# A trunk of gated attention layers: the value projections of two attentions as seven block products, values parked in DRAM, and a softmax difference in one operation

## The chip, the cores and the metric

The kernel runs on one core of a Trainium2 chip. The metric is the time of one execution on the device, in microseconds (us). Before the change, three runs gave 1922.32 us (median), 1922.04 us (lowest) and 1923.9 us (highest).

The engines are named as in the profile: PE is the matrix engine (TensorE), PEld its loading of the stationary operand, DVE the vector engine, ACT the scalar engine, POOL is GpSimd and SP is SyncE, which issues nearly all DMAs of this kernel.

## What is computed

Two layers over 512 tokens of width 1024. Each layer mixes tokens by three branches on the same input, and then applies a SwiGLU block that the change doesn't touch. Cut to what matters:

```
x                                     # (512, 1024)
in-projection of x:                   # one weight matrix w_in, column ranges
    rq, rk, rv, rg                    # retention: 512, 512, 1024, 1024 columns
    cq, ck, cv                        # chunked attention: 512 columns each, 8 heads of 64
    dq, dk, dv                        # differential attention: 512 columns each, 4 heads of 128
    gates                             # 3 branches x 1024 columns
A = retention(rq, rk, rv) * silu(rg)
B = chunked attention: softmax(cq ck' + bias) cv          # per head, under a triangle of chunks
C = differential attention, per head with two score matrices S0 and S1:
    o = (softmax(S0) - lam * softmax(S1)) dv
    o = o / sqrt(mean(o^2) + eps) * g * (1 - lambda_init)
mix = sum over branches of sigmoid(gate) * (branch @ w_branch)
x   = layer_norm(alpha * x + mix @ w_out)
```

## The kernel before

Every projection is made in three passes (lines 122, 123, 124): a float32 operand is split into a high part and a rest (tiles `wh` and `wl` for weights, `xTh` and `xTl` for the input), and high x high, rest x high and high x rest are added up in PSUM. The high part is a cast on ACT (line 106, or line 151 for weights that `Wt` loads and line 225 for those of `Halves`), the rest a subtraction on DVE (line 112, 152, 226). A matmul of the kernel mostly has 128 rows, a stationary operand of 128 columns and 512 moving columns.

The body of a layer is a hand-written list of items (at the end of the layer function). An item is one projection, with the weights that it needs, and up to a few groups of attention steps: the steps stand between the parts of the projection, so that PE has matmuls of the projection to do while ACT and DVE work on a softmax. Weights are loaded three items ahead (`AHEAD`) into three slots (`NSTAGE`). Engines take their instructions in the order in which the list and a recorder of the program put them; waits between engines go by semaphores. The items are:

- `u_gate(br, i)`: 256 gate columns, a tanh on ACT (line 965) into a tile `th`; the ones in `EARLY` are made long before use, stored to DRAM and loaded again.
- `u_rvg(hp)`: for one half of the retention heads, the 512 value and the 512 gate columns together as a product of a 2x2 block of inputs with a 2x2 block of weights, with seven block products in place of eight (Winograd's form: items m1, y, x, m2, v, g, h). `Halves` loads the weights' four quarters of 1 MB and makes the sums of quarters on DVE (line 182); `Quarters` holds the sums of the input's quarters. Each of the seven is 2 x 12 matmuls into banks named `pf`.
- `u_vhl(dst, base, wd)`: the 512 value columns of the chunked attention (`cv`) or the differential attention (`dv`) in the direct way, 4 x 24 matmuls into banks named `pn`. Each row block is cast and split into tiles `vhl`, where high part and rest of a head lie side by side.
- `u_cqk(p)`, `u_dqk(h)`: queries and keys of two heads of the chunked, or of one head pair of the differential attention, 24 matmuls for the queries and 24 for the keys. For the differential attention both are turned by `rotary` (lines 313 to 317): four copies `sw` on ACT, three operations on DVE; then `set_q` and `set_k` cast on ACT (`qs`, `ks`) and subtract on DVE (`kl`).
- `u_branch(br, i)`: 256 columns of a branch's output, multiplied by the gate and added up (lines 995 and 999).

The attention steps of the chunked attention are `s_c1` (scores into `psc`, maximum on DVE and exponential with sums on ACT at lines 363 and 365, then reciprocal and four multiplications of the tiles `cE` by it on DVE, line 829), `s_c2` (ten transposes into `ptr`, line 378, then casts `cPh` and rests `cPl`), and `s_c3` (product with the values, banks `pco`, line 854, a copy `cos` and an addition `cot`). Those of the differential attention are `s_d0(h, j)` for the two score matrices (lines 363, 365, reciprocal at 886, times -lam at 888), `s_d1` after the second (lines 901 and 902: for each of four row blocks, one multiplication of the second softmax and one operation that scales the first and adds), `s_d2` (ten transposes of `dE`, casts `dPh`), `s_d3` (product with the values, banks `pdo`, lines 927 to 944, with copies `do`, squares `junk` and the root mean square) and `s_d4` (four transposes `pdt`, line 954, and a split into `och` and `ocl`, which the last branch reads). The functions `c(i)` and `d(i)` say which steps belong to the i-th step of the pipeline: d(i) scores head i // 2 while the head before is transposed and multiplied.

In the list, the pairs of d steps stand with `u_gate(1, i)` and `u_branch(1, i)`, and between two pairs stands `u_dqk(h)` with no step at all:

```
(u_gate(1, 0), *d(0)), (u_branch(1, 0), *d(1)), (u_dqk(1),),
(u_gate(1, 1), *d(2)), (u_branch(1, 1), *d(3)), (u_dqk(2),),
```

Of the kernel before, what the change touches and what calls it, by code (L numbers as in the profile page):

```python
# [17 lines left out]
P = 128  # L18
# [25 lines left out]

EARLY = [(0, 0), (0, 1), (0, 2), (0, 3), (2, 0), (2, 1)]

# [10 lines left out]
def trunk(ctx, tc, x_in, xT_in, w_in, ret_norm_g, da_norm_g, lq1, lk1, lq2, lk2, w_a, w_b, w_c, b_merge, w_out,  # L57
# [100 lines left out]
    class Halves:  # L158
# [16 lines left out]

        def parts(self):
            h = max(self.kh // 2, 1)
            return [slice(a, min(a + h, self.kh)) for a in range(0, self.kh, h)]

        def add(self, t, u):  # L180
            for s in self.parts():
                nc.vector.tensor_add(t[:, s], t[:, s], u[:, s])

        def block(self, t):
            return Staged(t, self.kh, self.parts())

# [29 lines left out]
    class Staged:  # L216


        def __init__(self, st, nk, parts):
            n = 512 * nk  # L220
            self.nk = nk
            self.hi = wsp.tile([P, 2048], F32R, tag="wh", name="wh")[:, :n].rearrange("p (k c) -> p k c", k=nk)
            self.lo = wsp.tile([P, 2048], F32R, tag="wl", name="wl")[:, :n].rearrange("p (k c) -> p k c", k=nk)
            for s in parts:
                nc.scalar.copy(self.hi[:, s], st[:, s])  # L225
                nc.vector.tensor_sub(self.lo[:, s], st[:, s], f(self.hi[:, s]))  # L226

# [298 lines left out]
    def layer(l):  # L526
# [128 lines left out]

        def u_rvg(hp):

            hv = Halves(W, 0, 4, (RV + 512 * hp, RG + 512 * hp))
            t = {}
# [14 lines left out]
            def x(j, ps):  # L674
                u, y = g(name="tu"), t["y", j]
                t["u", j] = u
                nc.vector.tensor_sub(u, ps, t["m", j])
                nc.vector.tensor_add(y, y, u)

            def m2(j, ps):  # L680
                c = t.pop(("m", j))
                nc.vector.tensor_add(c, c, ps)
                rv_done(hp, j, c)

            def v(j, ps):
                c = g(name="tv")
                nc.vector.tensor_add(c, t["y", j], ps)
                rg_done(hp, j, c)

            def g_(j, ps):  # L690
                c, u = t.pop(("y", j)), t["u", j]
                nc.vector.tensor_add(c, c, ps)
                nc.vector.tensor_add(u, u, ps)
                rg_done(hp, 2 + j, c)

            def h(j, ps):
                u = t.pop(("u", j))
                nc.vector.tensor_sub(u, ps, u)
                rv_done(hp, 2 + j, u)

# [74 lines left out]

        def u_vhl(dst, base, wd):

            def fn(*wts):
                for t in range(NT):
                    ps = bank("pn")  # L780
                    proj_N(xT, wts, t, ps)
                    for hf in range(2):
                        s = g(F32R, "vhl")
                        dst[t, hf] = s
                        s3 = s.rearrange("p (h x) -> p h x", x=2 * wd)
                        src = ps[:, 256 * hf:256 * hf + 256].rearrange("p (h x) -> p h x", x=wd)
                        part_hi(s3[:, :, 0:wd], src)
                        part_lo(s3[:, :, wd:2 * wd], src, s3[:, :, 0:wd])
                    between()
            return rows_of(W, base), fn  # L790

# [22 lines left out]
        def s_c1(h):  # L814
            def fn():
# [10 lines left out]
                for nt in range(NT):  # L826
                    pk, c = PACK[NT - 1 - nt]
                    e = E[pk][:, c:c + P * (nt + 1)]
                    nc.vector.tensor_scalar_mul(e, e, r[:, nt:nt + 1])
                cE[h] = E  # L830
# [50 lines left out]
        def s_d0(h, j):  # L881
            def fn():
                e = [g(name="dE") for _ in range(3)]
                sums = softmax_num(dqk[h], j, tabs["mask"], e)
                r = small.tile([P, NT], F32, tag="rec", name="rec")
                nc.vector.reciprocal(r, sums)
                if j:
                    nc.vector.tensor_scalar_mul(r, r, v["nlam"])
                dE[h, j] = e, r
                if j:  # L890
                    s_d1(h)()
            return fn

        def s_d1(h):
            def fn():
                (E0, R0), (E1, R1) = dE.pop((h, 0)), dE.pop((h, 1))
                E, R = (E0, E1), (R0, R1)
                for nt in range(NT):
                    pk, c = PACK[NT - 1 - nt]
                    cs = slice(c, c + P * (nt + 1))  # L900
                    nc.vector.tensor_scalar_mul(E[1][pk][:, cs], E[1][pk][:, cs], R[1][:, nt:nt + 1])
                    nc.vector.scalar_tensor_tensor(E[0][pk][:, cs], E[0][pk][:, cs], R[0][:, nt:nt + 1],
                                                   E[1][pk][:, cs], op0=ALU.mult, op1=ALU.add)
                dE[h] = E[0]
            return fn

        def s_d2(h):
            def fn():
                dP[h] = triangle("dP")
                transpose_triangle(dE.pop(h), dP[h])  # L910
            return fn

        def s_d3(h):
            def fn():
                pT = dP.pop(h)
                ss = small.tile([P, NT], F32, tag="ss", name="ss")
# [103 lines left out]

        p, q = u_rvg(0), u_rvg(1)
        for (specs, fn), *groups in [
            (u_first(),), (u_gate(0, 1), [s_q(0)], [s_q(1)]), (p["m1"], [], [s_q(2)]),
            (u_gate(0, 2), [s_q(3)], [s_r1(0)]), (p["y"],), (p["x"],), (u_gate(0, 3), [], [s_r1(1)]), (p["m2"],), (p["v"],),
            (u_gate(2, 0),), (p["g"],), (p["h"],),
            (u_rqk(rq, RQ, 1), [], [s_r2(0)]), (q["m1"],), (u_rqk(rk, RK, 1), [s_r2(1)], [s_r3(0)]), (q["y"], [], [s_r3(1)]),
            (u_gate(2, 1),), (q["x"],), (q["m2"],), (q["v"],), (q["g"],), (q["h"],),
            (u_vhl(cv, CV, 64), [s_r1(2)], [s_r1(3)], [s_r2(2)], [s_r2(3)]), (u_cqk(0), [s_r3(2)], [s_r3(3)]),
            (u_branch(0, 0), *c(0)), (u_cqk(1), *c(1)), (u_branch(0, 1), *c(2)), (u_cqk(2), *c(3)),
            (u_branch(0, 2), *c(4)), (u_cqk(3), *c(5)), (u_branch(0, 3), *c(6)),  # L1030
            (u_vhl(dv, DV, 128), *c(7), *c(8)), (u_dqk(0), *c(9)),
            (u_gate(1, 0), *d(0)), (u_branch(1, 0), *d(1)), (u_dqk(1),),
            (u_gate(1, 1), *d(2)), (u_branch(1, 1), *d(3)), (u_dqk(2),),
            (u_gate(1, 2), *d(4)), (u_branch(1, 2), *d(5)), (u_dqk(3),),
            (u_gate(1, 3), *d(6)), (u_branch(1, 3), *d(7)), (u_gate(2, 2), [s_d4(2)], [s_d2(3)]),
            (u_gate(2, 3), [s_d3(3)], [s_d4(3)]),
# [274 lines left out]
```

## Time and profile before

| | before |
|---|---|
| three runs: median, lowest, highest | 1922.32, 1922.04, 1923.9 us |
| the profiled execution: its own time | 1923.79 us |
| the profiled execution: span of the core | 1922.0 us |
| mean granted clock of PE | 0.998 |
| busy: PE, PEld | 1907.8 us, 1606.2 us |
| busy: DVE, ACT, POOL | 1305.7 us, 876.8 us, 46.2 us |
| moved by DMA | 241.05 MB, mean 125 GB/s |

The span is the time from the first to the last instruction on the core; the profiled execution's own time has 1.8 us around it. Busy time of an engine is the time in which at least one of its instructions is under way. For PE it says little about speed, since matmuls overlap in the pipeline: a matmul's recorded duration is longer than the distance to the next one's start. The distance from start to start, in the timeline, is what one of a row of matmuls costs.

### The profile page before, as it was taken

To read this page: it belongs to the slowest core of one execution; us is meant where nothing else is said; L and a number is where in the kernel's file an instruction comes from. 1 tells how busy PE (TensorE), PEld (TensorE's weight loads), DVE (VectorE), ACT (ScalarE), POOL (GpSimd) and SP (SyncE) were. 2 spreads that over 40 slices of the span, in tenths; PEclk is the share of its full clock that TensorE was granted. 3 is DMA by queue.
4 is the path that set the end of the run, shared out by engine and by line. 5 is a ranking of instruction groups with operands and counts; after the bars stand their busy time and mean duration, and the time that the engine had idled before them with its cause. 6 is when DMAs were issued, how large, how long until landed. Compare 5 with 4: busy or idle time off the path is not lost. (4 is left out here: it accounts for less than half of the span.)

```text
span 1922.0 us, 23998 instructions
## 1 busy us (share of the span) xinstructions
PE 1907.8 (99%) x9250; PEld 1606.2 (84%) x9250; DVE 1305.7 (68%) x2183; ACT 876.8 (46%) x1551; POOL 46.2 (2%) x73
## 2 busy tenths in 40 slices
PE   9999999999999999999999999999999999999998
PEld 7888888888888888888898888888888898888886
DVE  7677766667765757666588776665776667675666
ACT  5444455567634333333255544554765343333331
POOL 0000000000000000000000000000000000000000
PEclk9999999999999999999999999999999999999999
DMA  7453343233154444434335444332221624444331
GB/s 251 168 171 121 121 135 112 57 94 97 44 183 125 148 137 127 137 109 143 121 140 185 156 138 135 113 95 92 77 87 62 202 78 153 148 137 132 110 127 48
DMA packets 242070, 241.05 MB, mean 125 GB/s; under 512 B 8366, under 2 KB 180516, under 8 KB 241956
## 3 DMA queue, kind: packets, MB, share of 16 engines
q1 hardware_dynamic: 241956, 239.52, 39.2%
q8 instruction: 72, 1.18, 0.3%
q14 instruction: 42, 0.34, 0.1%
HBM read 224.77 MB, written 14.73 MB: 125 GB/s over the span
## 5 line engine op out<-in xcount | busy, mean ns | idle before, releaser
L122 PE MATMUL pt<-xTh,wh 128*128 128x512 f32 (+1 forms) x1584 | 596.8, 377 | 1.5 <-ACT xTh L519 1.5
L123 PE MATMUL pt<-xTl,wh 128*128 128x512 f32 (+1 forms) x1584 | 593.6, 375 | 1.1 <-DVE xTl L520 1.1
L124 PE MATMUL pt<-xTh,wl 128*128 128x512 f32 (+1 forms) x1584 | 593.2, 375 | 0.0
L151 ACT CAST wh<-st 128x1024 fp32r<-128x1024 f32 (+1 forms) x282 | 268.6, 981 | 272.3 <-issue 138.8
L152 DVE TENSOR_TENSOR wl<-st,wh 128x1024 fp32r<-128x1024 f32 (+1 forms) x282 | 314.0, 1137 | 106.8 <-ACT wh L151 106.3
L123 PEld LDWEIGHTS pt<-xTl,wh 128*128 128x128 f32 x1584 | 298.8, 189 | 54.0 <-DVE xTl L520 2.1
L122 PEld LDWEIGHTS pt<-xTh,wh 128*128 128x128 f32 x1584 | 298.3, 189 | 54.4 <-ACT xTh L519 2.3
L124 PEld LDWEIGHTS pt<-xTh,wl 128*128 128x128 f32 x1584 | 298.4, 188 | 53.6
L225 ACT CAST wh<-st 128x1024 fp32r<-128x1024 f32 x64 | 64.9, 1051 | 97.6 <-PE pt L123 65.0
L1105 DVE TENSOR_TENSOR fth<-fth,pt 128x512 f32<-128x512 f32 x44 | 30.2, 686 | 104.4 <-PE pt L124 104.4
L225 ACT CAST wh<-sa 128x1024 fp32r<-128x1024 f32 x48 | 49.6, 1051 | 67.2 <-PE pt L123 64.0
L226 DVE TENSOR_TENSOR wl<-st,wh 128x1024 fp32r<-128x1024 f32 x64 | 76.6, 1221 | 5.3 <-ACT wh L225 5.1
L1103 ACT ACTIVATE fth<-pt 128x512 f32<-128x512 f32 x44 | 26.2, 596 | 107.7 <-PE pt L124 107.7
L313 ACT COPY sw<-pt 32x512 f32<-32x512 f32 (+1 forms) x96 | 55.6, 580 | 33.5 <-PE pt L124 26.5
L226 DVE TENSOR_TENSOR wl<-sa,wh 128x1024 fp32r<-128x1024 f32 x48 | 57.9, 1220 | 18.2 <-ACT wh L225 18.1
L1104 DVE SCALAR_TENSOR_TENSOR fth<-fth,pt 128x512 f32<-128x512 f32 x44 | 30.1, 685 | 58.0 <-ACT fth L1103 58.0
L365 ACT ACTIVATE cE<-cE,mx 128x512 f32<-128x512 f32 (+1 forms) x64 | 35.3, 553 | 38.7 <-DVE mx L363 38.4
L122 PE MATMUL pt<-oah,wh 128*128 128x512 f32 x128 | 51.2, 400 | 0.0
L122 PE MATMUL pn<-wh,xTh 128*128 128x512 f32 x128 | 50.4, 394 | 0.0
L123 PE MATMUL pt<-oal,wh 128*128 128x512 f32 x128 | 50.1, 392 | 0.2
L124 PE MATMUL pt<-oah,wl 128*128 128x512 f32 x128 | 50.0, 391 | 0.0
L122 PE MATMUL pf<-wh,s12h 128*128 128x512 f32 x128 | 50.0, 390 | 0.0
(280 smaller groups left out, 3484.8 us busy)
## 6 DMA issues: line engine op xcount, KB each, us to landing
st<-in_w_in SPq DMA_DIRECT2D x63, 1024.0 KB
st<-in_w_ffn_in SPq DMA_DIRECT2D x88, 512.0 KB
st<-in_w_ffn_out SPq DMA_DIRECT2D x28, 1024.0 KB
st<-in_w_in SPq DMA_DIRECT2D x32, 512.0 KB
th<-th SPq DMA_DIRECT2D x48, 256.0 KB
st<-in_w_branch_a SPq DMA_DIRECT2D x8, 1024.0 KB
st<-in_w_out SPq DMA_DIRECT2D x8, 1024.0 KB
saved<-z SPq DMA_DIRECT2D x24, 256.0 KB
```

What stands on the lines that cost most here:

```text
L122: nc.tensor.matmul(ps, lh, rh, start=start, stop=False)
L123: nc.tensor.matmul(ps, lh, rl, start=False, stop=False)
L124: nc.tensor.matmul(ps, ll, rh, start=False, stop=stop)
L151: done = [nc.scalar.copy(self.hi[:, a:b], st[:, a:b]), nc.vector.tensor_sub(self.lo[:, a:b], st[:, a:b], f(self.hi[:, a:b]))]
L152: nc.vector.tensor_sub(self.lo[:, a:b], st[:, a:b], f(self.hi[:, a:b]))]
L225: nc.scalar.copy(self.hi[:, s], st[:, s])
L226: nc.vector.tensor_sub(self.lo[:, s], st[:, s], f(self.hi[:, s]))
L313: nc.scalar.copy(sw[half * b:half * b + half], ps[half * o:half * o + half])
L365: nc.scalar.activation(e, e, AF.Exp, bias=m, scale=-1.0, accum_out=sums[:, nt:nt + 1])
L1103: nc.scalar.activation(t, pg, AF.Tanh, scale=0.5)
L1104: nc.vector.scalar_tensor_tensor(t, t, 1.0, pg, op0=ALU.add, op1=ALU.mult)
L1105: nc.vector.tensor_mul(t, t, pu)
```

## The change

It has three parts, and an order of items that goes with them.

1. The value projections of the chunked and of the differential attention, before two direct products of 4 x 24 matmuls each, become one product `w` of a 2x2 block of weights (columns of `cv` on the left, of `dv` on the right) by the seven products that `u_rvg` used; that function becomes `u_two(left, right, left_done, right_done)`. The product stands early in the layer. Its results are split into `vhl` tiles as before, stored to DRAM (`v_away`) and loaded again (`v_back`) shortly before the attention that needs them: 16 tiles of 256 KB per layer, out and back.
2. The softmax difference: the reciprocal of the second sums, times the first sums, times -lam, is one factor per row; one operation per row block then gives E0 + factor x E1, not divided by the first sums. The root mean square that follows makes up for the missing division, with the first sums squared times eps in place of eps.
3. The four multiplications of `cE` in `s_c1` go from DVE to ACT; sums and splits of weight quarters in `Halves` and `Staged` are made in one instruction of 2048 columns each, before in two of 1024.

In the list of items, `u_gate(1, 0)` comes before the chunked attention and its tile waits in DRAM too (`EARLY`), and the `u_dqk` items carry attention steps now.

```
-EARLY = [(0, 0), (0, 1), (0, 2), (0, 3), (2, 0), (2, 1)]
+EARLY = [(0, 0), (0, 1), (0, 2), (0, 3), (1, 0), (2, 0), (2, 1)]
...
         def add(self, t, u):
-            for s in self.parts():
-                nc.vector.tensor_add(t[:, s], t[:, s], u[:, s])
+            nc.vector.tensor_add(t, t, u)
...
-            for s in parts:
-                nc.scalar.copy(self.hi[:, s], st[:, s])
-                nc.vector.tensor_sub(self.lo[:, s], st[:, s], f(self.hi[:, s]))
+            nc.scalar.copy(self.hi, st)
+            nc.vector.tensor_sub(self.lo, st, f(self.hi))
...
-        def u_rvg(hp):
-            hv = Halves(W, 0, 4, (RV + 512 * hp, RG + 512 * hp))
+        def u_two(left, right, left_done, right_done):
+            hv = Halves(W, 0, 4, (left, right))
...
             def m2(j, ps):
-                c = t.pop(("m", j))
-                nc.vector.tensor_add(c, c, ps)
-                rv_done(hp, j, c)
+                c = g(name="tm")
+                nc.vector.tensor_add(c, t["m", j], ps)
+                left_done(j, c)
...
+        def v_away(dst, wd):
+            def done(t, c):
+                for hf in range(2):
+                    s = g(F32R, "vhl")
+                    s3 = s.rearrange("p (h x) -> p h x", x=2 * wd)
+                    src = c[:, 256 * hf:256 * hf + 256].rearrange("p (h x) -> p h x", x=wd)
+                    part_hi(s3[:, :, 0:wd], src)
+                    part_lo(s3[:, :, wd:2 * wd], src, s3[:, :, 0:wd])
+                    dst[t, hf] = dram.tile([P, 512], F32, name=f"v{l}_{wd}_{t}_{hf}")
+                    nc.sync.dma_start(dst[t, hf], f(s))
+            return done
+        def v_back(dst):
+            def fn():
+                for k, away in list(dst.items()):
+                    dst[k] = g(F32R, "vhl")
+                    nc.sync.dma_start(f(dst[k]), away)
+            return fn
...
-                    nc.vector.tensor_scalar_mul(e, e, r[:, nt:nt + 1])
+                    nc.scalar.mul(e, e, r[:, nt:nt + 1])
...
-                    nc.vector.tensor_scalar_mul(E[1][pk][:, cs], E[1][pk][:, cs], R[1][:, nt:nt + 1])
-                    nc.vector.scalar_tensor_tensor(E[0][pk][:, cs], E[0][pk][:, cs], R[0][:, nt:nt + 1],
-                                                   E[1][pk][:, cs], op0=ALU.mult, op1=ALU.add)
+                nc.vector.reciprocal(R, S1)
+                nc.vector.tensor_mul(R, R, S0)
+                nc.vector.tensor_scalar_mul(R, R, v["nlam"])
+                    nc.vector.scalar_tensor_tensor(E0[pk][:, cs], E1[pk][:, cs], R[:, nt:nt + 1], E0[pk][:, cs],
+                                                   op0=ALU.mult, op1=ALU.add)
...
-                nc.vector.tensor_scalar(ss, ss, c2 / P, c2 * LN_EPS, op0=ALU.mult, op1=ALU.add)
+                nc.vector.scalar_tensor_tensor(sums, sums, c2 * LN_EPS, sums, op0=ALU.mult, op1=ALU.mult)
+                nc.vector.scalar_tensor_tensor(ss, ss, c2 / P, sums, op0=ALU.mult, op1=ALU.add)
...
-            (u_gate(1, 0), *d(0)), (u_branch(1, 0), *d(1)), (u_dqk(1),),
-            (u_gate(1, 1), *d(2)), (u_branch(1, 1), *d(3)), (u_dqk(2),),
-            (u_gate(1, 2), *d(4)), (u_branch(1, 2), *d(5)), (u_dqk(3),),
-            (u_gate(1, 3), *d(6)), (u_branch(1, 3), *d(7)), (u_gate(2, 2), [s_d4(2)], [s_d2(3)]),
+            (u_branch(0, 2), *c(4)), (u_cqk(3), *c(5)), (u_branch(0, 3), *c(6)), (u_dqk(0), *c(7)),
+            (u_gate(1, 1), *c(8)), (u_dqk(1), [s_c3(7), v_back(dv)], d(0)[1]), (u_branch(1, 0), *d(1)),
+            (u_gate(1, 2), *d(2)), (u_dqk(2), *d(3)), (u_branch(1, 1), *d(4)), (u_dqk(3), *d(5)),
+            (u_branch(1, 2), *d(6)), (u_gate(1, 3), *d(7)), (u_branch(1, 3),), (u_gate(2, 2), [s_d4(2)], [s_d2(3)]),
```

Where the order of instructions moves, three places follow. First PE at the step of the differential attention in which a head pair's difference is transposed. Before, between the second scores `psc` of a head pair and the transposes `ptr` of their difference stood a whole `u_dqk` item (48 matmuls) and the first half of the next gate (24). The rows of before show the end of that stretch:

```order
L122 MATMUL pt<-xTh,wh 128x512
L123 MATMUL pt<-xTl,wh 128x512
L124 MATMUL pt<-xTh,wl 128x512
L954 MATMUL pdt<-ident,do 128x128 x4
L378 MATMUL ptr<-ident,dE 128x128 x10
L122 MATMUL pt<-xTh,wh 128x512
L123 MATMUL pt<-xTl,wh 128x512
L124 MATMUL pt<-xTh,wl 128x512
```

So 72 matmuls of projections stand between the scores and the transposes there. After, at the same place (in `u_dqk(2)` and `u_branch(1, 1)`, where `pt<-obh,wh` is the branch's product):

```order
L343 MATMUL psc<-kl,qs 128x128
L122 MATMUL pt<-obh,wh 128x512
L123 MATMUL pt<-obl,wh 128x512
L124 MATMUL pt<-obh,wl 128x512
L122 MATMUL pt<-obh,wh 128x512
L123 MATMUL pt<-obl,wh 128x512
L124 MATMUL pt<-obh,wl 128x512
```

Twelve such matmuls stand behind the scores after the change, and then `pdt` (4) and `ptr` (10) follow; ahead of the scores stand the 24 matmuls of the key half of `u_dqk(2)`.

The second place is ACT in that step. Before:

```order
L365 ACTIVATE dE,sums<-dE,mx 128x128
L313 COPY sw<-pt 32x512 x4
L108 ACTIVATE qs<-rot 64x512 x2
L151 CAST wh<-st 128x1024
L313 COPY sw<-pt 32x512 x4
L151 CAST wh<-st 128x1024
L106 CAST ks<-rot 64x512 x4
L965 ACTIVATE th<-pt,hb 128x512
L108 ACTIVATE och<-pdt,colv 128x512
L106 CAST dPh<-ptr 128x512 x2
```

and after:

```order
L151 CAST wh<-st 128x512
L307 COPY sw<-pt 32x512 x4
L151 CAST wh<-st 128x512
L106 CAST ks<-rot 64x512 x4
L359 ACTIVATE dE,sums<-dE,mx 128x512
L108 ACTIVATE och<-pdt,colv 128x512
L359 ACTIVATE dE,sums<-dE,mx 128x384
L359 ACTIVATE dE,sums<-dE,mx 128x256
L359 ACTIVATE dE,sums<-dE,mx 128x128
L106 CAST dPh<-ptr 128x512 x2
```

The four exponentials `dE,sums` stood ahead of the keys' copies `sw` and casts `ks`; now they stand behind them, and the casts of the transposes directly after. The same order comes again one head later (`u_dqk(3)` and `u_branch(1, 2)`).

The third place is ACT at `u_dqk(0)`, where head 6 of the chunked attention is transposed and multiplied while head 7 is scored. Before, the casts `cPh` of a head's transposes stood there ahead of any copy of the keys:

```order
L106 CAST vhl<-pn 128x2x128
L106 CAST cPh<-ptr 128x512 x2
L106 CAST cP<-ptr 128x256
L313 COPY sw<-pt 32x512 x4
L108 ACTIVATE qs<-rot 64x512 x2
```

After, the exponentials of head 7, the keys' copies and casts, and the four multiplications that moved from DVE (line 828) stand ahead of head 6's `cPh`:

```order
L359 ACTIVATE cE,sums<-cE,mx 128x128
L307 COPY sw<-pt 32x512
L828 ACTIVATE cE<-cE,rec 128x128
L828 ACTIVATE cE<-cE,rec 128x256
L828 ACTIVATE cE<-cE,rec 128x384
L828 ACTIVATE cE<-cE,rec 128x512
L307 COPY sw<-pt 32x512 x3
L151 CAST wh<-st 128x512
L106 CAST ks<-rot 64x512 x4
L106 CAST cPh<-ptr 128x512 x2
```

More of the change, by code (lines that the diff above doesn't have):

```diff
@@ L174, in load @@
             return t
-        def parts(self):
-            h = max(self.kh // 2, 1)
-            return [slice(a, min(a + h, self.kh)) for a in range(0, self.kh, h)]
         def add(self, t, u):
-            for s in self.parts():
-                nc.vector.tensor_add(t[:, s], t[:, s], u[:, s])
+            nc.vector.tensor_add(t, t, u)
         def block(self, t):
-            return Staged(t, self.kh, self.parts())
+            return Staged(t, self.kh)
         def b11(self):
@@ L216, in trunk, with __init__ @@
     class Staged:
-        def __init__(self, st, nk, parts):
+        def __init__(self, st, nk):
             n = 512 * nk
@@ L773, in s_r3 @@
             return fn
[L776 to L790, printed above, removed]
+        def v_away(dst, wd):
[15 more added lines that the diff above has]
+            return fn
         def v_of(dst, mt, h, wd):
@@ L883, in fn @@
                 e = [g(name="dE") for _ in range(3)]
[L884 to L889, printed above, removed]
+                dE[h, j] = e, softmax_num(dqk[h], j, tabs["mask"], e)
                 if j:
@@ L895, in fn @@
             def fn():
-                (E0, R0), (E1, R1) = dE.pop((h, 0)), dE.pop((h, 1))
-                E, R = (E0, E1), (R0, R1)
+                (E0, S0), (E1, S1) = dE.pop((h, 0)), dE.pop((h, 1))
+                R = small.tile([P, NT], F32, tag="rec", name="rec")
+                nc.vector.reciprocal(R, S1)
+                nc.vector.tensor_mul(R, R, S0)
+                nc.vector.tensor_scalar_mul(R, R, v["nlam"])
                 for nt in range(NT):
@@ L908, in fn @@
             def fn():
-                dP[h] = triangle("dP")
-                transpose_triangle(dE.pop(h), dP[h])
+                E, sums = dE.pop(h)
+                dP[h] = triangle("dP"), sums
+                transpose_triangle(E, dP[h][0])
             return fn
@@ L914, in fn @@
             def fn():
-                pT = dP.pop(h)
+                pT, sums = dP.pop(h)
                 ss = small.tile([P, NT], F32, tag="ss", name="ss")
```

29 lines of the change are left out of this document (15 added, 14 removed).

## The prediction

> **What bounds the kernel now.** I read the page's busy times first, then PE's waits, then PE's timeline where it does wait, and then the timelines of PE, ACT and DVE around one step of the differential attention.
>
> ```profile
> span 1922.0 us, 23998 instructions
> PE 1907.8 (99%) x9250; PEld 1606.2 (84%) x9250; DVE 1305.7 (68%) x2183; ACT 876.8 (46%) x1551; POOL 46.2 (2%) x73
> q1 hardware_dynamic: 241956, 239.52, 39.2%
> ```
>
> ```profile
> engine line waited for: us in total, times, longest us
> PE pt L122 <- ACT xTh L519: 1.5, 2, 1.2
> PE warm L507 <- POOL ident masks.py:199: 1.5, 1, 1.5
> PE pt L123 <- DVE xTl L520: 1.1, 2, 0.8
> PE pco L854 <- DVE cPl L112: 0.7, 2, 0.3
> PE px L435 <- DVE z L426: 0.5, 2, 0.3
> ```
>
> PE is under way for 99% of the span and all its waits add up to 5.3 us. So a matmul that goes is time saved, work taken from DVE or ACT is worth nothing by itself, and the one way to lose is to make PE wait. Busy times don't give a matmul's price. The timeline of PE early in the run does (start, duration, instruction, wait):
>
> ```profile
> 15.40 0.39 PE L123 MATMUL pt<-xTl,wh 128*128 128x512 f32 x1
> 15.63 0.39 PE L124 MATMUL pt<-xTh,wl 128*128 128x512 f32 x1
> 17.27 0.50 PE L122 MATMUL pt<-xTh,wh 128*128 128x512 f32 x1 [1.25 <-ACT xTh L519]
> 18.61 0.50 PE L123 MATMUL pt<-xTl,wh 128*128 128x512 f32 x1 [0.84 <-DVE xTl L520]
> 18.95 0.58 PE L124 MATMUL pt<-xTh,wl 128*128 128x512 f32 x1
> 19.32 0.63 PE L122 MATMUL pt<-xTh,wh 128*128 128x512 f32 x1
> 19.75 0.63 PE L123 MATMUL pt<-xTl,wh 128*128 128x512 f32 x1
> ...
> 21.89 0.63 PE L122 MATMUL pt<-xTh,wh 128*128 128x512 f32 x1
> 22.31 0.45 PE L123 MATMUL pt<-xTl,wh 128*128 128x512 f32 x1
> 22.59 0.40 PE L124 MATMUL pt<-xTh,wl 128*128 128x512 f32 x1
> ```
>
> Undisturbed matmuls start 0.23 us apart (15.40, 15.63), though each lasts 0.39. After two short waits (1.25 and 0.84 us) they start 0.43 us apart from 18.95 to 22.31, and then 0.28 and less: half the rate for 3.4 us, which loses about 1.7 us. So a wait of PE can cost more than itself.
>
> **The saving.** Two value projections of 4 x 24 matmuls become seven products of 24: 192 - 168 = 24 matmuls fewer per layer, 48 in all. The exact distance is taken from a longer row of them:
>
> ```profile
> 424.05 0.39 PE L122 MATMUL pt<-xTh,wh 128*128 128x512 f32 x1
> 429.49 1.25 PE L378 MATMUL ptr<-ident,dE 128*128 128x128 f32 x10
> 430.50 0.48 PE L122 MATMUL pt<-xTh,wh 128*128 128x512 f32 x1
> 436.06 0.39 PE L348 MATMUL psc<-ks,qs 128*128 128x512 f32 x1
> 437.27 0.44 PE L122 MATMUL pt<-obh,wh 128*128 128x512 f32 x1
> 440.07 0.28 PE L927 MATMUL pdo<-vhl,dPh 128*128 128x256 f32 x1
> ```
>
> From 424.05 to 429.49, 24 matmuls take 5.44 us, 0.227 each; 48 are **10.9 us**. The same rows price what stands between: ten transposes 1.01 us (429.49 to 430.50), four then 0.40; a set of scores 1.21 (436.06 to 437.27); twelve branch matmuls 2.80 (437.27 to 440.07).
>
> **What DVE and ACT gain or lose.** Groups by line (count, busy us, mean ns):
>
> ```profile
> L829 DVE TENSOR_SCALAR cE<-cE,rec 128x128 f32<-128x128 f32 (+1 forms) x64 | 20.6, 382 | 0.6
> L901 DVE TENSOR_SCALAR dE<-dE,rec 128x128 f32<-128x128 f32 (+3 forms) x32 | 10.9, 382 | 0.3
> L902 DVE SCALAR_TENSOR_TENSOR dE<-dE,rec 128x128 f32<-128x128 f32 (+3 forms) x32 | 16.1, 545 | 0.0
> L888 DVE TENSOR_SCALAR rec<-rec,nlam 128x4 f32<-128x4 f32 x8 | 1.8, 230 | 0.3
> L225 ACT CAST wh<-st 128x1024 fp32r<-128x1024 f32 x64 | 64.9, 1051 | 97.6 <-PE pt L123 65.0
> L226 DVE TENSOR_TENSOR wl<-st,wh 128x1024 fp32r<-128x1024 f32 x64 | 76.6, 1221 | 5.3 <-ACT wh L225 5.1
> ```
>
> DVE loses 20.6 us of `cE` multiplications (to ACT) and 10.9 us of `dE` ones. Since PE waits for none of these lines, I credit nothing. The merged casts and splits hand over 2048 columns at once: about 2 x 1.05 us of cast and then 2 x 1.22 of rest, so the first half arrives some 2.3 us later than before. PE's long runs of products in the retention part hide it now; without that cover it would be 2.3 us for each of a layer's blocks. The early part of a layer now has three products of seven with little attention between, DVE nearly as long at work there as PE; I bound its loss at 0 and 5 us per layer, and take 1 for it and the chunked steps together, near the waits view's small rows. The values' way through DRAM is 16 stores and 16 loads of 256 KB per layer on SP's queue, which is in use 39% of the span; reloading `dv` has some 100 matmuls (over 20 us) before its first reader. I cost it at nothing; if SP's queue is held up by a tile that isn't free, the weights behind it are late, and that would be a wait on DMA.
>
> **Where the change makes PE wait.** The step of the differential attention after `u_dqk(2)`, and again after `u_dqk(3)`. The rows of ACT and DVE at the same step before:
>
> ```profile
> 411.85 1.14 ACT L151 CAST wh<-st 128x512 fp32r<-128x512 f32 x2 [1.90 <-PE pt L123]
> 425.74 2.35 ACT L313 COPY sw<-pt 32x512 f32<-32x512 f32 x4
> 431.24 2.55 ACT L106 CAST ks<-rot 64x512 fp32r<-64x512 f32 x4 [2.07 <-DVE rot L317]
> 433.81 0.69 ACT L965 ACTIVATE th<-pt,hb 128x512 f32<-128x512 f32 x1
> 434.40 1.07 ACT L106 CAST dPh<-ptr 128x512 fp32r<-128x512 f32 x2
> ...
> 438.50 0.72 ACT L365 ACTIVATE dE<-dE,mx 128x512 f32<-128x512 f32 x1
> 440.32 0.39 ACT L365 ACTIVATE dE<-dE,mx 128x128 f32<-128x128 f32 x1
> 442.28 0.29 ACT L937 ACTIVATE junk<-do 128x128 f32<-128x128 f32 x1
> ```
>
> ```profile
> 440.83 0.18 DVE L886 RECIPROCAL rec<-sums 128x4 f32<-128x4 f32 x1
> ```
>
> The key half of `u_dqk(1)` left PE at 424.05 (call it T). Its cast `ks` ended at 433.79, T + 9.7: ACT came to `sw` 1.7 us late, copied for 2.35, waited for DVE's rotation, cast for 2.55. `dPh` started only at 434.40, behind `ks` and `th`, though its transposes were over at 430.50: ACT takes its queue in order. Before, that hurt nobody: PE wanted `dPh` at 440.07, and the exponentials were far ahead, with 72 matmuls (16.4 us) between scores and transposes.
>
> After, ACT's queue has `sw`, a cast, `ks`, and only then the exponentials, with `och` among them. The way to the last transpose:
> - `ks` ends between T + 7.5 and T + 9.2: the 9.7 of before, less 0.5 as the cast in between has 512 columns now (0.57 for 1.05), and at best less the 1.7 of lateness.
> - Four exponentials: 2.2 us (438.50 to 440.71). `och`, a 128x512 form as `th`: 0.7.
> - On DVE the reciprocal 0.18, the new product of two 128x4 tiles (not in the trace; between 0.18 and 0.23 by its neighbours), times -lam 0.23: 0.6.
> - Four operations of line 902's kind, 4 x 0.545 = 2.2 less small overlaps: 2.1.
> - The transposes left behind the last of them, about 7 of 10: 0.7.
>
> Sum 6.3, so the transposes end between T + 13.8 and T + 15.5. PE gets there after scores, 12 matmuls, `pdt` and ten transposes: 1.21 + 2.80 + 0.40 + 1.01 = T + 5.4. The wait is 8.4 to 10.1 us; I take **9.3**, the middle, twice per layer. Behind it on PE stands everything else, and nothing makes up for it, as PE is the bound.
>
> Two smaller ones of the same kind, once per layer each:
> - At `u_dqk(0)`, head 6's `cPh` stands on ACT behind a weight cast (0.57; it reuses the slot that the key half has just read, so it starts at T), head 7's exponentials (2.2), `sw` (2.35), the four moved multiplications, a cast or DVE's rotation (about 1.3) and `ks` (2.55). The multiplications on ACT aren't in the trace: 4 x 0.29 to 4 x 0.69 us by the squares and `th`, or 1.5 at DVE's speed (4 x 0.382); I take 1.7. With 0.6 for the first cast that is T + 11.3, and up to 1.2 more where PE wants `cPl` as well. PE comes to `pco` after 10 transposes and 24 matmuls, T + 6.5. Wait 4.5 to 7, taken **5.9**.
> - At `u_dqk(1)` and `u_branch(1, 0)`, a weight cast holds ACT's queue until the branch's first use of a slot is over, T + 6.7 (scores and 24 matmuls), then come `ks`, both sets of exponentials and the difference: 0.57 + 2.55 + 2 x 2.2 + 2.7, T + 17; PE wants the first transposes at 6.7 + 1.2 + 5.4 = T + 13.3. **3.7**, between 1.8 (if half of the exponentials get ahead) and 5.5.
>
> After each of the two long waits I add the 1.7 us of half rate seen above: 4 x 1.7 = 6.8.
>
> [...]
>
> **The sum**, against the profiled execution's own 1923.8: - 10.9 + 2 x (9.3 + 9.3 + 5.9 + 3.7 + 1) + 6.8 = - 10.9 + 58.4 + 6.8, which gives 1978.1. The median of the runs is 1.5 below that execution, so **1977**. With every term at its lower bound and no half rate, 2 x (16.8 + 4.5 + 1.8) = 46.2 gives 1957.6; with every term at its upper bound and half rate after all four waits, 2 x (20.2 + 7 + 5.5 + 5) + 13.6 = 89 gives 2000.4.
>
> **Rivals.**
> - *The chains fit under PE, and only the saving is left:* 1922.3 - 10.9 = **1911**. For it speaks that ACT is busy 46% and that nearly no wait of PE is seen now. Against it stands `dPh` at 434.40, behind `ks`. It decides if the waits of a layer sum to less than 5.4 us; one of the two long ones alone is estimated higher. Chance 0.07.
> - *The two long waits come, the two smaller ones and the half rate don't,* since casts of that place get ahead: 2 x 16.8 = 33.6, **1945**. For it: the slots' order decides when a weight cast may start, which I took from the order of instructions, not from a trace. Chance 0.15.
> - *The values are late too:* the three early products keep DVE behind, or SP's queue holds up weights, more than the upper bound's 5 us per layer: over 2000, say **2006**. For it: a merged split is 2.3 us later. Against: PE waited for none before. Chance 0.07.
> - *The change doesn't save what it says:* PE waits for the sums and splits of the new product as long as its missing matmuls took, and the other waits are small: within 4 us of **1922**. Chance 0.03.
>
> **How the numbers follow.** The forecast, 1958 to 2000, has 0.68. About 0.2% (4 us) is what a measurement of this kernel can tell from no change. Slower is the forecast with the second and third rival, 0.90; same 0.03; faster 0.07. The range takes in the forecast's bounds and the second rival with some room: 1938 to 2002.
>
> **What would show it.** Right: PE waits on `ptr` for DVE's `dE` (after's line 899) in the waits view, twice per layer, 8 to 10 us each in several pieces, with ACT at `sw` and `ks` in that time; a wait on `pco` for `cPh` or `cPl` of 5 to 6 us once per layer; half-rate matmuls for 3.4 us behind them; PE's matmuls 48 fewer. Wrong: exponentials that run on ACT before `ks`, waits on `ptr` under 3 us, waits on `wh` or `wl` in the retention part, or waits on DMA.

## The result, and the profile after

The changed kernel takes 2008.22 us (median of 4 runs, 2007.57 to 2009.22), the kernel before 1923.11 us on the same chip (4 runs): a ratio of 1.0443, 95% interval 1.0425 to 1.0461. It is slower by 85 us; the forecast was 1977 with a range up to 2002.

The page of the changed kernel, and its table of PE's waits (us in total, times, longest):

```profile
span 2006.4 us, 23998 instructions
PE 1920.9 (96%) x9202; PEld 1609.9 (80%) x9202; DVE 1315.6 (66%) x2041; ACT 912.4 (45%) x1565; POOL 44.2 (2%) x73
```

```profile
PE ptr L372 <- DVE dE L899: 33.4, 4, 8.4
PE pco L853 <- ACT cPh L106: 14.1, 4, 6.5
PE psc L342 <- DVE mx L357: 7.7, 4, 3.0
PE psr L122 <- DVE rtmp L716: 5.4, 2, 2.7
PE pt L122 <- DVE rtmp L716: 4.9, 2, 2.4
PE pco L853 <- DVE cPl L112: 4.0, 7, 0.8
PE pf L122 <- ACT s12h L106: 3.0, 1, 3.0
```

PE has 48 matmuls fewer, as counted, and the total of its waits has gone from 5.3 to 76.9 us (all rows of the table; those above are 72.5). The span grew by 84.4 us though 10.9 us of matmuls are gone, so 95.3 us were lost: 71.6 in these waits, and the remaining 23.7 mostly in matmuls that start slower behind them (0.43 us apart from 136.93 to 139.92, in place of 0.227). The profile gives the granted clock of any stretch of time: it is 0.50 at ten places of the changed kernel, for 64.9 us together, in which PE is busy 41.0 (not counting the last 6 us of the span, where the kernel before has it too). Half of that, 20.5 us, is an estimate of what the half clock costs. None of PE's waits is for a DMA.

**The differential attention.** ACT's timeline at the first of the two long waits of layer 0 (`u_dqk(2)` with `u_branch(1, 1)`), then PE's and two rows of DVE's:

```profile
486.89 2.35 ACT L307 COPY sw<-pt 32x512 f32<-32x512 f32 x4
...
491.86 2.54 ACT L106 CAST ks<-rot 64x512 fp32r<-64x512 f32 x4 [1.97 <-DVE rot L311]
494.42 0.72 ACT L359 ACTIVATE dE<-dE,mx 128x512 f32<-128x512 f32 x1
...
496.93 0.39 ACT L359 ACTIVATE dE<-dE,mx 128x128 f32<-128x128 f32 x1
```

```profile
489.64 0.60 PE L953 MATMUL pdt<-ident,do 128*128 128x128 f32 x4
498.62 2.62 PE L372 MATMUL ptr<-ident,dE 128*128 128x128 f32 x10 [8.38 <-DVE dE L899]
500.89 0.78 PE L122 MATMUL pt<-obh,wh 128*128 128x512 f32 x1
501.47 0.63 PE L123 MATMUL pt<-obl,wh 128*128 128x512 f32 x1
501.89 0.50 PE L124 MATMUL pt<-obh,wl 128*128 128x512 f32 x1
```

```profile
493.12 0.68 DVE L357 CUSTOM_DVE_ANT_0 dE<-psc,mask 128x512 f32<-128x512 f32 x1
...
498.12 1.94 DVE L899 SCALAR_TENSOR_TENSOR dE<-dE,rec 128x128 f32<-128x128 f32 x4
```

ACT goes from `sw` at 486.89 to `ks`, and only at 494.42 to the exponentials, whose scores PE had made before 486.84. DVE's queue has the same order: the maximum of the scores (line 357), which the first exponential needs, ran at 493.12, behind the keys' rotation and the first `kl`, and ended at 493.8, 0.6 us before ACT got to it. So the keys held up both queues. PE has `pdt` done at 490 and gets the first transpose at 498.62. The ten transposes then take 2.27 us (to 500.89) in place of 1.01: partly in step with DVE's four operations, partly at half the clock (granted: 0.50 from 495.30 to 502.12), as the branch matmuls behind them show by 0.58 and 0.42 between starts.

**The retention part.** DVE's timeline in the part where the three products of seven stand close together, then PE's:

```profile
130.23 0.68 DVE L716 TENSOR_TENSOR rtmp<-psr,dh 128x512 f32<-128x512 f32 x1
132.35 2.29 DVE L220 TENSOR_TENSOR wl<-sa,wh 128x2048 fp32r<-128x2048 f32 x1 [1.44 <-ACT wh L219]
134.56 0.69 DVE L112 TENSOR_TENSOR rpl<-rtmp,rph 128x512 fp32r<-128x512 f32 x1
135.16 0.75 DVE L716 TENSOR_TENSOR rtmp<-psr,dh 128x384 f32<-128x384 f32 x2
```

```profile
135.76 0.39 PE L122 MATMUL psr<-rqkh 128*128 128x256 f32 x1 [2.72 <-DVE rtmp L716]
```

PE's scores of the retention (`psr`) need a bank that DVE's second `rtmp` must first read. Ahead of that `rtmp` in DVE's queue stands the split of a merged block, which first waits 1.44 us for ACT's merged cast and then runs 2.29 us. This is the same shape as in the attention: a short operation that PE wants, behind a long one that it doesn't want yet.

### The profile page after: what moved, and what is told of

Same layout as the page of the kernel before. It is cut to its first block, busy times and chain, and to the rows that moved or that the text cites. A ratio compares the mean times of both kernels' runs of the same rounds, so it can differ in the third digit from the quotient of the medians.

```text
span 2006.4 us, 23998 instructions
## 1 busy us (share of the span) xinstructions
PE 1920.9 (96%) x9202; PEld 1609.9 (80%) x9202; DVE 1315.6 (66%) x2041; ACT 912.4 (45%) x1565; POOL 44.2 (2%) x73
## 5 line engine op out<-in xcount | busy, mean ns | idle before, releaser
L152 DVE TENSOR_TENSOR wl<-st,wh 128x1024 fp32r<-128x1024 f32 (+1 forms) x266 | 295.8, 1132 | 91.0 <-ACT wh L151 79.7
L219 ACT CAST wh<-st 128x2048 fp32r<-128x2048 f32 x40 | 76.5, 1914 | 124.5 <-PE pt L123 82.6
L220 DVE TENSOR_TENSOR wl<-st,wh 128x2048 fp32r<-128x2048 f32 x40 | 91.5, 2290 | 52.6 <-ACT wh L219 52.4
L219 ACT CAST wh<-sa 128x2048 fp32r<-128x2048 f32 x30 | 57.4, 1912 | 73.2 <-PE pt L123 52.8
L220 DVE TENSOR_TENSOR wl<-sa,wh 128x2048 fp32r<-128x2048 f32 x30 | 68.7, 2291 | 33.3 <-ACT wh L219 33.1
L123 PE MATMUL pf<-wl,s12h 128*128 128x512 f32 x160 | 64.0, 401 | 0.0
L124 PE MATMUL pf<-wh,s12l 128*128 128x512 f32 x160 | 63.1, 399 | 0.2 <-DVE s12l L112 0.2
L122 PE MATMUL pf<-wh,s43h 128*128 128x512 f32 x160 | 62.2, 389 | 0.0
L123 PE MATMUL pf<-wl,s43h 128*128 128x512 f32 x160 | 62.2, 389 | 0.0
L124 PE MATMUL pf<-wh,s43l 128*128 128x512 f32 x160 | 62.2, 389 | 0.0
```

Of the source, the lines that this page charges most:

```text
L122: nc.tensor.matmul(ps, lh, rh, start=start, stop=False)
L123: nc.tensor.matmul(ps, lh, rl, start=False, stop=False)
L124: nc.tensor.matmul(ps, ll, rh, start=False, stop=stop)
L152: nc.vector.tensor_sub(self.lo[:, a:b], st[:, a:b], f(self.hi[:, a:b]))]
L219: nc.scalar.copy(self.hi, st)
L220: nc.vector.tensor_sub(self.lo, st, f(self.hi))
```

## The experiments

**One place repaired at a time.** Four runs each take the changed kernel and undo or move one thing. The first two change where steps stand in the list:

```
-            (u_gate(1, 2), *d(2)), (u_dqk(2), *d(3)), (u_branch(1, 1), *d(4)), (u_dqk(3), *d(5)),
+            (u_gate(1, 2), *d(2)), (u_dqk(2), d(3)[0] + d(3)[1]), (u_branch(1, 1), *d(4)), (u_dqk(3), d(5)[0] + d(5)[1]),
```

> The changed kernel with one move: in u_dqk(2) and u_dqk(3) the scores and exponentials of the second softmax go into the first group of steps, so PE makes them before the key half and ACT's exponentials stand ahead of the keys' sw and ks. Theory (ACT's queue: the exponentials wait behind sw and ks): the four waits of PE on ptr for dE, 8.4 us each, shrink to about 1 us, and the half-rate matmuls behind them go; with 9.5 us saved at each of four places, 2008 - 38 = about 1970 us. Rival (too few matmuls between scores and transposes, wherever ks stands): the move puts 24 more matmuls there, worth 5.4 us each, so waits of 3 us remain: 2008 - 22 = about 1986 us.

Measured: 1984.48 us, 23.7 less. Of PE's waits, and DVE's row of the difference at the place shown above:

```profile
PE ptr L372 <- DVE dE L899: 4.6, 13, 0.8
PE psc L342 <- DVE th L994: 3.2, 4, 0.8
PE psc L342 <- ACT ks L106: 1.2, 2, 0.6
```

```profile
489.98 1.94 DVE L899 SCALAR_TENSOR_TENSOR dE<-dE,rec 128x128 f32<-128x128 f32 x4
```

The time is the rival's. Of 33.4 us on `ptr` 4.6 are left, about 1.2 at each place, as the theory of ACT's queue had it, not 3 us. What the theory missed is the next wait. The keys now stand behind the exponentials, and the next scores (`psc`) wait for `ks` and for the branch's `th` instead, neither of which is in the changed kernel's table. The move changes two things at once, and the traces part them. From the end of the scores to the end of the difference the changed kernel takes 13.1 us (487.0 to 500.06), and this one 10.5 (481.45 to 491.92): the order in the queues of ACT and DVE takes 2.6 us off. PE's work between scores and transposes grows from 3.2 to 8.7 us, by the 24 matmuls that now stand there: 5.4 us. So the larger part of the gain at this place is the rival's distance, and the smaller one the queues' order.

The second moves the transposes of chunked head 6:

```
-            ... (u_branch(0, 3), *c(6)), (u_dqk(0), *c(7)),
+            ... (u_branch(0, 3), *c(6)), (u_dqk(0), [s_c3(5), s_c2(6), s_c1(7)]),
```

> The changed kernel with one move: in u_dqk(0) the transposes of chunked head 6 are made before the key half, so ACT's casts cPh stand ahead of the keys' sw and ks and of head 7's exponentials. Theory (ACT's queue again): the wait of 6.5 us on pco for cPh and the 2.5 us of short waits and half rate around it go, in both layers: 2008 - 2 x 8.5 = about 1991 us. Rival (the four multiplications of cE on ACT are what makes head 6 late): cE of head 6 is then late for its transposes too, PE waits on ptr, and under 5 us are saved: above 2003 us.

Measured: 2000.7 us, 7.5 less: less than half of what the theory forecast, and more than the rival allowed. PE's waits, and the end of the new one:

```profile
PE pt L122 <- DVE cot L856: 7.4, 2, 3.7
PE pco L853 <- ACT cPh L106: 1.1, 2, 0.6
```

```profile
405.50 0.79 PE L122 MATMUL pt<-xTh,wh 128*128 128x512 f32 x1 [3.70 <-DVE cot L856]
```

Of the waits for `cPh`, 14.1 us in the changed kernel, 1.1 are left, and PE waits for a bank that `cot` has to free; `cot` needs ACT's `cos`, which now stands behind the queries' work. Behind the new wait matmuls start 0.44 us apart on average, from 405.50 to 410.79, and 0.24 from 411.20 on. The theory named the right queue and overlooked the neighbour.

The third brings `parts()` back, so that sums, casts and splits of weight quarters have 1024 columns each:

```
         def add(self, t, u):
-            nc.vector.tensor_add(t, t, u)
+            for s in self.parts():
+                nc.vector.tensor_add(t[:, s], t[:, s], u[:, s])
...
-            nc.scalar.copy(self.hi, st)
-            nc.vector.tensor_sub(self.lo, st, f(self.hi))
+            for s in parts:
+                nc.scalar.copy(self.hi[:, s], st[:, s])
+                nc.vector.tensor_sub(self.lo[:, s], st[:, s], f(self.hi[:, s]))
```

> The changed kernel with the sums and splits of weight quarters made in two instructions of 1024 columns again (56 + 32 more instructions on ACT and DVE, same work). Theory (the 2.3 us instructions stand in DVE's queue ahead of the short operations rtmp and sa that PE waits for): the waits of PE before 160 us and at 1128 to 1145 us, 13.7 and 6.6 us with their half rate against 1.2 and 1.2 before, shrink to a third or less: 2008 - 12 to - 17, about 1994 us. Rival (three products in a row simply give DVE as much work as PE, and order within it doesn't matter): 2006 to 2010 us, the waits stay where they are.

Measured: 1991.42 us, 16.8 less, at the theory's upper end. The rows of `rtmp` are gone from PE's waits, and `s12h` has 0.4 us left. (By its page this kernel has 70 more instructions on ACT and 110 more on DVE than the changed one.)

The fourth puts the multiplications of `cE` back on DVE:

```
-                    nc.scalar.mul(e, e, r[:, nt:nt + 1])
+                    nc.vector.tensor_scalar_mul(e, e, r[:, nt:nt + 1])
```

> The changed kernel with the four multiplications of cE in each chunked head made on DVE again. Theory (on ACT they stand ahead of the casts cPh that PE wants, 1.9 us a head): the waits on pco for cPl and cPh in the pair steps at 324 to 327, 355 to 357 and 385 us go (3.3 us a layer), and the wait at u_dqk(0) shrinks by 1.9 us: 2008 - 2 x 5 = about 1998 us. Rival (DVE has no room there and gives the time back): 2005 to 2010 us.

Measured: 1996.57 us, 11.7 less, as the theory had it. `cPl` has 0.2 us left, and `cPh` is down from 14.1 to 9.5.

**All of the list at once.** The next two have a list in the manner of before: `u_dqk(1)` to `u_dqk(3)` without steps, `u_gate(2, 0)` and `u_gate(2, 1)` no longer early, so that they can carry steps:

```
-EARLY = [(0, 0), (0, 1), (0, 2), (0, 3), (1, 0), (2, 0), (2, 1)]
+EARLY = [(0, 0), (0, 1), (0, 2), (0, 3), (1, 0)]
...
+            (u_branch(0, 2), *c(4)), (u_cqk(3), *c(5)), (u_branch(0, 3), *c(6)), (u_gate(2, 0), *c(7)),
+            (u_dqk(0), [s_c3(6), s_c2(7)]), (u_gate(1, 1), [s_c3(7), v_back(dv)], *d(0)[1:]), (u_branch(1, 0), *d(1)), (u_dqk(1),),
+            (u_gate(1, 2), *d(2)), (u_branch(1, 1), *d(3)), (u_dqk(2),),
+            (u_gate(1, 3), *d(4)), (u_branch(1, 2), *d(5)), (u_dqk(3),),
+            (u_gate(2, 1), *d(6)), (u_branch(1, 3), *d(7)), (u_gate(2, 2), [s_d4(2)], [s_d2(3)]),
```

The first of them has halves and the multiplications on DVE as well; what stays of the change is the product of the values, their way through DRAM, the softmax difference, and `u_gate(1, 0)` made early.

> The changed kernel's values product, storing, reloading and softmax difference, with a list of items like that of before (u_dqk(1) to u_dqk(3) without steps; gate(2,0) and gate(2,1) made late to carry steps), sums and splits in halves and the cE multiplications on DVE. Theory (the 48 matmuls are saved in full, and all the loss came from order, merged blocks and the move to ACT): 1923 - 10.9 + 0 to 4, between 1912 and 1916 us. Rival (the product of the values itself, or its way through DRAM, costs what it saves): 1920 us or more, with waits of PE in the first 70 us of a layer or waits on a DMA of vhl.

Measured: 1912.24 us against 1922.8 (ratio 0.9943, interval 0.9928 to 0.9958): the theory, and faster than both kernels. Its page:

```profile
span 1910.8 us, 24155 instructions
PE 1896.7 (99%) x9202; PEld 1597.5 (84%) x9202; DVE 1339.5 (70%) x2215; ACT 893.3 (47%) x1571; POOL 46.2 (2%) x73
```

PE's waits add up to 5.2 us, as before (5.3), and the largest row has 1.5. DVE works 24 us longer than in the changed kernel, in 174 instructions more, and the kernel is 96 us faster.

> The changed kernel with only the list of items as in the run before it: merged blocks and the cE multiplications on ACT stay. Theory (the list's loss is the four places where exponentials, casts and scores wait behind the keys' work, 36 us a layer): 2008 - 2 x 36 = about 1936 us, with the waits on rtmp and in the chunked steps left. Rival (the two gates that now come late were what gave DVE time in the retention part): waits there grow, above 1945 us.

Measured: 1950.36 us, the rival's side. The long waits of the four places are gone, and the retention part is worse than in the changed kernel:

```profile
PE prt L763 <- DVE ro L750: 6.4, 2, 3.5
PE psr L122 <- DVE rtmp L716: 5.4, 2, 2.7
PE pf L122 <- DVE rtmp L716: 5.0, 4, 1.6
PE pco L853 <- DVE cPl L112: 4.5, 8, 0.8
PE pf L122 <- DVE tm L676: 1.9, 2, 0.9
```

So with merged blocks the two gates among the products did give DVE room. Two more runs part that kernel's loss:

> The run with the new list alone (1950 us) and halves again for sums and splits; the cE multiplications stay on ACT. In that run PE waited 19 us for ro, rtmp and tm of the retention part and 6 us for cPh and cPl in the chunked steps, with half rate behind them. Theory (the merged blocks make the first group late, the move to ACT the second): 1950 - 28 = about 1922 us, waits on pco left as they are. Rival (either one alone takes up the slack, and the other hides it): less than 15 us saved, above 1935 us.

Measured: 1919.95 us, 30.4 less, with `ro`, `tm` and nearly all of `rtmp` gone from the waits, and `cPl` (4.4 us) and `cPh` (1.1) left: the theory.

> The run with the new list alone (1950 us) and the cE multiplications on DVE again; merged blocks stay. Theory: the waits on pco go, those on rtmp, ro and tm stay: 1950 - 8 = about 1942 us. Rival (DVE gets 20 us more work in the chunked part and runs late with merged blocks): 1948 us or more.

Measured: 1944.14 us (two runs, 1942.28 and 1946.01), 6.2 less, where the two runs of each kernel lie some 4 us apart: nearer the theory, with the size known only roughly. The two repairs together gave 38.1 (to 1912.24), and one by one 30.4 and 6.2: within that spread they add up.

**Parts of the change in the kernel before.** Each part alone, put into the old kernel:

> The kernel before with one part of the change: sums and splits of weight quarters in one instruction of 2048 columns. Theory (a 2.3 us instruction hurts only where DVE has as much work as PE, as with three products in a row; before, gates and branches lie between): 1923 to 1927 us. Rival (the long instruction delays rtmp, sa and the first half of every block anywhere): 1930 to 1940 us, with waits on rtmp as in the changed kernel.

Measured: 1924.44 us over 10 runs, ratio 1.0009 (1.0000 to 1.0019): the theory. The same merge that costs 30 us in the new list costs 1.6 us in the old one, 0 to 3.7 by the interval. The old list has fewer merged blocks, with gates and direct products between them; which of its differences does it was not run by itself.

> The kernel before with one part of the change: the softmax difference in one operation per row block, 11 us less on DVE. Theory (DVE's saving is hidden behind PE): 1921 to 1924 us, no change. Rival (the reciprocal and factors that now come after the second exponentials lengthen the way to the transposes, and PE waits on ptr): 1925 us or more.

Measured: 1922.93 us over 10 runs, ratio 1.0000 (0.9990 to 1.0009): no change, the theory.

**The softmax difference where PE does wait.**

> The changed kernel with the softmax difference of before (two operations per row block). Theory (DVE's work counts where PE waits for it: the four multiplications of line 901's kind, 1.2 to 1.5 us a head pair, lie on the way to the transposes at four places): 2008 + 4 x 1.3 = about 2013 us, with waits of 9.5 us on ptr in place of 8.4. Rival (they run while DVE waits for the last exponentials anyway): 2007 to 2010 us.

Measured: 2014.11 and 2025.45 us. Both lie above 2008, but 11 us apart, too far to size 5 us by; the profiled run is the slower one, and in it the wait on `ptr` is

```profile
PE ptr L372 <- DVE dE L901: 36.7, 8, 8.6
```

3.3 us more than the 33.4 of the changed kernel. That speaks for the theory's direction; its size stays open. Of the 17.3 us by which the profiled run lies above the changed kernel's, 4.9 are waits (81.8 against 76.9). The half clock makes up most of the rest: PE is busy 64.9 us at 0.50 here and 41.0 there (mean granted clock 0.975 and 0.982), by estimate about 12 us of loss more.

**The changed kernel's own list, with all small repairs.** Scores before keys also in `u_dqk(1)`, and the four repairs above together:

> The changed kernel's own list with every repair so far and one more: scores before the keys in u_dqk(1), u_dqk(2) and u_dqk(3), transposes before the keys in u_dqk(0), halves, cE on DVE. Theory (repairs add up, but u_dqk items with steps hold more of ACT's work than their 48 matmuls cover, so part of the waits only moves): 2008 - 24 - 7 - 17 - 12 = 1948, less up to 12 for u_dqk(1): 1936 to 1948 us, above the 1912 us that u_dqk items without steps gave. Rival (the waits left in the first two runs came from merged blocks and ACT's multiplications): below 1925 us.

Measured: 1961.39 us, more than either forecast. The move in `u_dqk(1)`, which no run before had, made a new long wait. PE's waits, and DVE at that place:

```profile
PE ptr L378 <- DVE dE L905: 22.6, 14, 9.0
```

```profile
444.20 1.33 DVE L1000 SCALAR_TENSOR_TENSOR th<-th,pt 128x512 f32<-128x512 f32 x2 [1.97 <-DMA th<-th]
...
446.64 0.17 DVE L899 RECIPROCAL rec<-sums 128x4 f32<-128x4 f32 x1
```

The second exponentials still wait behind the keys there, and DVE then waits 1.97 us for the stored gate to come back from DRAM, with the softmax difference behind it. So the repairs tried within the changed list took 47 us of the loss and moved part of the waits, while the list without steps in `u_dqk` has none of these waits. Another order within the changed list may do better; none beyond these was tried.

## Why the prediction was wrong, point by point

**Right: the saving.** 48 matmuls at 0.227 us. With the rest of the loss removed, 1912.24 against 1922.8 us is 10.6, beside 10.9 forecast.

**Right: the two long waits.** Forecast 9.3 us each, four times 37.2; measured 33.4 on `ptr` for `dE`, where the prediction looked for it. `ks` ended at 494.40, 8.8 us after the key half (485.6), between the bounds of 7.5 and 9.2. That the place of the scores is the cause is shown by the run that moves only them: 4.6 of the 33.4 us stayed. The prediction's account has both of its parts, the chain through the queues and the few matmuls on PE beside it. It followed ACT's queue alone; DVE's maxima were held up nearly as long.

**Right in size, one step early: the wait at `u_dqk(1)`.** 7.7 us over both layers, 3.85 each for 3.7 forecast. But PE stands at `psc`, one step ahead of the transposes named: the banks of the scores are full until DVE, with the keys ahead in its queue, has taken their maxima (`PE psc <- DVE mx`, 3.0 us at the longest).

**A little too small: `u_dqk(0)`.** Forecast 5.9, between 4.5 and 7; the two longest waits on `cPh` are 6.5 each, with `cPl` behind. ACT's queue there:

```profile
410.50 0.72 ACT L359 ACTIVATE cE<-cE,mx 128x512 f32<-128x512 f32 x1 [0.83 <-DVE mx L357]
413.30 1.92 ACT L828 ACTIVATE cE<-cE,rec 128x128 f32<-128x128 f32 x4
419.55 2.52 ACT L106 CAST ks<-rot 64x512 fp32r<-64x512 f32 x4 [1.92 <-DVE rot L311]
422.10 1.07 ACT L106 CAST cPh<-ptr 128x512 fp32r<-128x512 f32 x2
```

The moved multiplications took 1.92 us for 1.7 assumed, and the exponentials began later than the one cast allowed for.

**The step that failed: "The early part of a layer".** The prediction took 1 us per layer for the retention part and the chunked steps together, with a bound of 5, and said of the merged blocks that "PE's long runs of products in the retention part hide it now". PE's waits there are 5.4 + 4.9 + 3.0 us in the retention part and 4.0 on `cPl` with the short ones (1.1) on `cPh` in the chunked steps, 18 us in place of 2, and half rate came on top (granted clock 0.50 from 78.87 to 85.70 and from 136.90 to 140.31). The runs give their causes: halves in place of merged blocks took 16.8 us off the changed kernel and 30.4 with the other list; `cE` on DVE took 11.7 and 6.2. The prediction had weighed how much work DVE and ACT have against PE, and had asked how late a block itself becomes. What decided was how long the block's two instructions keep a short operation behind them waiting, and what the moved multiplications hold up on ACT. The run that puts the merge into the kernel before shows that the cover was real there. That the three products in a row took it away is argued from the lists and not shown by a run of its own; that the waits there grew from 13.3 to 18.7 us without the two gates points the same way.

**The second failed term: half rate.** 6.8 us were taken, for four waits; 23.7 us were lost beyond the waits themselves, by estimate some 20 of them by the half clock. The prediction gave half rate only to the two long waits of a layer. It came there, at `u_dqk(0)` and `u_dqk(1)` of both layers, and twice in the first layer's early part: ten places. Half rate was seen behind shorter waits too (2.72 and 2.98 us), and at seven of the ten places for longer than the 3.4 us taken: 6.83 or 10.24 (below).

**The upper end.** In 2000.4 stood 5 us per layer for the early part and 13.6 for half rate, 1.7 after each of four waits a layer. No run shows the 13.6; the changed kernel's trace shows half clock at ten places, some 20 us of loss by the estimate above. The waits at the named places stayed below their upper bounds, 54.1 against 65.4. With the two terms as they turned out, the forecast's own other steps reach the measured time: 1977 less the 2 and 6.8 taken for them, plus 13.3 for the retention part, about 5 for the chunked steps and 23.7, is 2010.

**The rivals.** "The values are late too", given 0.07 and over 2000 us, names the region in which the time fell. Its mechanism was half right: merged splits kept DVE behind in the early part. DMA had no part in it on PE's side.

## What to carry to other kernels

When a list of items is rearranged, read for each engine's queue what long or waiting instruction comes to stand ahead of a short one that the bounding engine wants; a balance of busy times does not show it (DVE was busy 68% of the span before and 66% after). Merging instructions saved little here (two splits of 1024 columns took 2 x 1.22 us, one of 2048 took 2.29) and made what stands behind them wait longer: that cost 1.6 us in the kernel before, 16.8 in the changed one and 30.4 with the other list. And where a change has several parts, measure them apart: here the one that saved 10.9 us was good, and the moves and merges around it cost 95.

## What the hardware showed beyond what was expected

Half rate followed waits shorter than thought, and mostly lasted longer than the 3.4 us taken. In the changed kernel's trace the granted clock is 0.50 in ten spells: three of 3.41 us, five of 6.83 and two of 10.24. First a row of PE's timeline, then stretches of the same trace (start and end, length, PE's busy time and matmuls, granted clock, and two columns on DMA):

```profile
79.53 0.80 PE L122 MATMUL pf<-wh,s12h 128*128 128x512 f32 x1 [2.98 <-ACT s12h L106]
```

```profile
78.87:82.29 3.42, 2.76 (x7) 0.50 0.25 96
82.29:85.70 3.41, 3.41 (x10) 0.50 0.63 171
85.70:89.11 3.41, 3.41 (x16) 1.00 0.58 218
...
147.14:150.55 3.41, 1.75 (x8) 1.00 0.00 0
150.55:153.97 3.42, 2.65 (x12) 1.00 0.67 212
...
495.30:498.71 3.41, 0.09 (x1) 0.50 0.05 16
498.71:502.12 3.41, 3.41 (x13) 0.50 0.00 0
```

The length of a wait alone did not decide. The 2.43 us that end at 151.32 fall into the stretches from 147.14 to 153.97 and brought no half clock: it is 1.00 in both. In the run with `cE` on DVE the same wait on `rtmp` was again 2.4 us long, and half clock followed:

```profile
149.64:153.06 3.42, 3.42 (x10) 0.50 0.78 274
```

What tells the two apart was not shown by a run of its own. The 2.72 us that end at 135.76 brought 3.41 us of half clock, from 136.90 on. The spell at the 8.38 us begins at 495.30, while PE still waits; of its 6.83 us only 3.5 slow any matmul. A longer wait thus did not always cost more by half clock: the 2.98 us above cost more, with PE busy 6.2 us in their spell. For a price per wait, an estimate from these rows, half of PE's busy time at 0.50: none or 1.7 us of loss after a wait of 2.4 us, and up to about 3 us after one of 3 us.
